# One plain block fewer per FFN, a third pair of rounded weights, and weight sums made by adding transfers

## The chip, the cores and the metric

The kernel runs on one core of a Trainium2 chip. The metric is the time of one execution in device microseconds (us). The engines named below are TensorE (PE in the rows; PEld is its weight load), VectorE (DVE), ScalarE (ACT), GpSimd (POOL) and SyncE (SP), which only sends transfers.

## The reference, cut to what matters

Two layers of a decoder trunk on 512 tokens, with 16 learned meta tokens in front, width 1024. Each layer has an attention part (two groups of heads, one output projection) and a SwiGLU FFN of width 2816. The change touches the FFN:

```python
hn = rmsnorm(h, ffn_norm_g)
ff = jax.nn.silu(jnp.einsum('bld,df->blf', hn, w_gate)) * jnp.einsum('bld,df->blf', hn, w_up)
return h + jnp.einsum('blf,fd->bld', ff, w_down)
```

Everything is float32. `w_gate` and `w_up` are 1024 × 2816 per layer, `w_down` 2816 × 1024.

## The kernel before, in words

**Layout.** The hidden state lies transposed: eight tiles `h[k]` of 128 channels by 528 tokens. Layer 0 works on all 528 columns in two halves of 264; layer 1, whose meta tokens nobody needs after attention, on 512, in plain blocks as one 512-wide matmul and elsewhere as two halves of 256.

**Precision.** A float32 product is made of three matmuls with rounded parts (fp32r): high weight by high x, high weight by low x, low weight by high x. A weight block of 128 columns is loaded into `raw` (or `fraw`) by SP; ACT makes the high part `whi` by a cast (L191 for plain blocks, L869 for units), and VectorE, or POOL in some attention stages, the low part `wlo` by subtraction (L194, L870). Plain blocks use the pair whi/wlo with two buffers, units take turns between whi/wlo and fwhi/fwlo.

**FFN.** The 22 blocks f of 128 FFN columns are grouped in ROUNDS. Those with f < PLAIN are plain: gate and up, each eight k-blocks times three matmuls times two halves, 96 half-width matmuls in all (L217). All others are a `Unit`: gate and up of both token halves as one two-by-two block product by the Winograd form of Strassen's method, with seven products of four k-blocks in place of eight, 84 half-width matmuls (L881). A unit's x-side operands are plain x blocks and four sums (`x_forms`, one call for each k of 0 to 3). `x_forms(k)` scales h[k] on ACT into `S`, makes four sums there on VectorE (L843, L845, L846) and splits them into `th` (ACT) and `tl` (VectorE, L143). All units of a layer share these forms. The weight-side operands come from `make1` to `make4`: the gate block as it is, and sums of halves of `w_gate` and `w_up`, written to `S`, over `fraw` and over `raw` (L915, L916, L922, L929), each followed by cast and subtraction. `need(j)` makes a weight operand when a product starts, and those of the next two jobs with it.

**Rounds.** Products on plain x come first in a unit (its head), then those on the forms. The down projection of the round before (L1016) is laid between the parts of the units. A unit without such a down part leaves its last products (its tail) until behind the head of the next unit.

**Start of an FFN.** The squares for the normalization are inserted at step 4 of the first gate block, `rstd` (the sum over channels on TensorE, L290, and Newton steps on VectorE, L297) at step 12, and the four `x_forms` from step 12 on, nine steps apart.

**Order.** TensorE's order is the order of the program, written by hand. The orders of the other engines are set by the tile scheduler when the program is built, by the order and the priority in which the program gives out the work, and are then fixed. Each engine works through its queue in that order and waits at an instruction until its operands and its buffer are there.

## Time and profile before

| what | value |
|---|---|
| median of three runs (lowest, highest) | 1271.39 us (1270.4, 1271.77) |
| profiled execution, its own time | 1271.32 us |
| its span | 1269.5 us |
| TensorE busy in the span | 1255.6 us |
| VectorE busy | 997.3 us |
| ScalarE busy | 687.7 us |
| GpSimd busy | 264.0 us |

The span is the profiled part of an execution; its own time is 1.8 us longer. The rows of the prediction give a start, or a window, in us from the start of the span. A group's row has its busy time and the number of its instructions. In rows of one engine the two numbers are start and length; since operations of one engine overlap a little at their ends, what one costs its queue is the distance to the next start. Lines (L217) are those of the kernel before.

### The profile page before, as it was taken

The numbers are of one execution on the slowest core, as the hardware profiler recorded it, in microseconds if no ns is written. First come the engines' busy times: TensorE is split into PE (matmuls) and PEld (weight loads), VectorE is DVE, ScalarE is ACT, GpSimd is POOL, SyncE is SP. The second block draws the span as 40 slices with busy tenths as digits, with TensorE's granted clock in tenths as the row PEclk, the third lists the DMA queues.
The fourth block names the chain that finished last, engine by engine and source line by source line (L and its number), as shares of the span: only waits on it lengthen the run. The fifth ranks groups of instructions, "written<-read, shape, count | busy, mean of one in ns | idle before, by whom it ended". The sixth has DMA issues, their size and how long they took to land.

```text
span 1269.5 us, 23615 instructions
## 1 busy us (share of the span) xinstructions
PE 1255.6 (99%) x9271; PEld 1197.8 (94%) x9271; DVE 997.3 (79%) x1843; ACT 687.7 (54%) x1246; POOL 264.0 (21%) x522
## 2 busy tenths in 40 slices
PE   9999999999999999999999999999999999999997
PEld 8999999999999999999999989998789999999996
DVE  7877756779988888887786877567899888888866
ACT  6666545676444444444456665557764444444444
POOL 3355546420000000000025545454100000000000
PEclk9999999999999999999999999999999999999999
DMA  6222232223333333332323232222323333333321
GB/s 217 93 69 86 88 87 73 70 68 114 107 97 100 100 100 101 100 100 84 101 76 119 62 99 83 80 88 68 101 95 120 100 100 100 101 100 100 104 80 67
DMA packets 45680, 120.57 MB, mean 95 GB/s; under 512 B 5360, under 2 KB 12272, under 8 KB 45568
## 3 DMA queue, kind: packets, MB, share of 16 engines
q1 hardware_dynamic: 45104, 118.74, 29.8%
q8 instruction: 73, 1.20, 0.4%
q10 hardware_dynamic: 464, 0.32, 0.1%
q14 instruction: 39, 0.32, 0.1%
HBM read 116.91 MB, written 2.13 MB: 94 GB/s over the span
## 4 chain that ended last, share of the span: by engine, by line
PE 94%; DVE 3%; ACT 2%; DMA 1%; issue 0%; DVEq 0%; ACTq 0%
PE psd L217 30%; PE psa L881 18%; PE psd L1016 14%; PE psd L881 13%; PE psa L217 5%; PE psa L1016 4%; PE psa L418 2%; PE psa L573 2%; PE psa L507 2%; PE psa L730 1%; PE psa L700 1%; PE psa L379 1%; PE psa L290 0%; ACT whi L191 0%; DMA raw<-w_in 0%
## 5 line engine op out<-in xcount | busy, mean ns | idle before, releaser
L194 POOL TENSOR_TENSOR wlo<-raw,whi 128x128 fp32r<-128x128 f32 x504 | 258.8, 548 | 288.5 <-ACT whi L191 288.4
L217 PE MATMUL psd<-xh,whi 128*128 128x264 f32 (+1 forms) x792 | 196.2, 315 | 0.6 <-ACT whi L191 0.6
L217 PE MATMUL psd<-xh,wlo 128*128 128x264 f32 (+1 forms) x792 | 187.2, 304 | 0.0
L217 PE MATMUL psd<-xl,whi 128*128 128x264 f32 (+1 forms) x792 | 186.7, 303 | 0.4 <-DVE xl L320 0.4
L217 PEld LDWEIGHTS psd<-xh,whi 128*128 128x128 f32 x792 | 128.9, 190 | 5.7 <-ACT whi L191 1.3
L217 PEld LDWEIGHTS psd<-xh,wlo 128*128 128x128 f32 x792 | 127.5, 189 | 6.2 <-DVE wlo L194 0.4
L217 PEld LDWEIGHTS psd<-xl,whi 128*128 128x128 f32 x792 | 128.0, 189 | 4.8 <-DVE xl L320 0.8
L191 ACT CAST whi<-raw 128x512 fp32r<-128x512 f32 (+1 forms) x168 | 98.3, 613 | 49.5 <-PE psd L217 37.6
L869 ACT CAST whi<-raw 128x1024 fp32r<-128x1024 f32 (+2 forms) x62 | 54.9, 885 | 51.2 <-PE psd L881 39.9
L869 ACT CAST fwhi<-raw 128x1024 fp32r<-128x1024 f32 (+2 forms) x62 | 55.7, 898 | 47.5 <-PE psd L881 39.9
L1116 POOL TENSOR_TENSOR th<-th,e 128x544 f32<-128x544 f32 x1 | 1.4, 1366 | 359.2 <-DVE e L1136 359.2
L870 DVE TENSOR_TENSOR wlo<-raw,whi 128x1024 fp32r<-128x1024 f32 (+2 forms) x62 | 62.9, 1015 | 12.9 <-ACT whi L869 12.8
L85 POOL MEMSET kl<- 64x528 f32 x2 | 1.1, 534 | 345.4 <-PE psa L881 345.4
L870 DVE TENSOR_TENSOR fwlo<-raw,fwhi 128x1024 fp32r<-128x1024 f32 (+2 forms) x62 | 64.0, 1032 | 10.5 <-ACT fwhi L869 10.3
L881 PE MATMUL psa<-th,whi 128*128 128x264 f32 (+1 forms) x232 | 65.4, 282 | 0.0
L881 PE MATMUL psa<-th,wlo 128*128 128x264 f32 (+1 forms) x232 | 65.4, 282 | 0.0
L881 PE MATMUL psa<-tl,whi 128*128 128x264 f32 (+1 forms) x232 | 65.3, 282 | 0.0
L881 PE MATMUL psa<-th,fwhi 128*128 128x264 f32 (+1 forms) x224 | 63.4, 283 | 0.0
L881 PE MATMUL psa<-tl,fwhi 128*128 128x264 f32 (+1 forms) x224 | 63.3, 283 | 0.0
L881 PE MATMUL psa<-th,fwlo 128*128 128x264 f32 (+1 forms) x224 | 63.2, 282 | 0.0
L527 ACT ACTIVATE probs<-probs,nmax 128x144 f32<-128x144 f32 (+1 forms) x64 | 36.9, 576 | 44.2 <-DVE nmax L514 31.3
L947 ACT COPY e<-psa 128x264 f32<-128x264 f32 (+1 forms) x114 | 42.9, 376 | 28.3 <-PE psa L881 24.1
(340 smaller groups left out, 4030.2 us busy)
## 6 DMA issues: line engine op xcount, KB each, us to landing
raw<-w_in SPq DMA_DIRECT2D x54, 512.0 KB, 3.5
raw<-w_gate SPq DMA_DIRECT2D x44, 512.0 KB, 3.7
fraw<-w_up SPq DMA_DIRECT2D x38, 512.0 KB, 3.5
raw<-w_down SPq DMA_DIRECT2D x64, 256.0 KB, 2.8
raw<-w_out SPq DMA_DIRECT2D x16, 512.0 KB, 3.4
raw<-w_down SPq DMA_DIRECT2D x32, 192.0 KB, 2.4
bc<-cdr SPq DMA_DIRECT2D x16, 264.0 KB, 3.5
raw<-w_up SPq DMA_DIRECT2D x6, 512.0 KB, 3.5
```

The lines of the kernel that those rows point to most:

```text
L191: pin(nc.scalar.copy(hi, job["raw"][:, c0:c1]), pinned)
L194: pin(sub(lo[:, i:i + step], job["raw"][:, c0 + i:c0 + i + step], hi[:, i:i + step].bitcast(F32)), pinned)
L217: nc.tensor.matmul(ps[1][b][:, 0:c1 - c0], w[:, wk, :], x[:, c0:c1], start=(k == 0 and i == 0), stop=(k == n - 1 and i == 2))
L418: nc.tensor.transpose(ps[:, 128 * j:128 * j + 128], src[:, o:o + 128], idt)
L507: nc.tensor.matmul(sc[0:nq, 0:c1 - c0], st["q"][s][:, q0:q0 + nq], kk[:, c0:c1], start=(i == 0), stop=(i == 1))
L527: nc.scalar.activation(pr, pr, AF.Exp, bias=nmax[0:nq], scale=-1.0, accum_out=rsum)
L573: nc.tensor.matmul(po[:, c0:SEQ], v[:, j, :], pp[:, j, META + c0:T], start=(j == 0 and i == 0), stop=(j == 4 and i == 1))
L869: nc.scalar.copy(hi, src)
L870: nc.vector.tensor_sub(lo, src, hi.bitcast(F32))
L881: nc.tensor.matmul(bank()[:, 0:b.shape[-1]], a[:, o + k, :], b, start=(fresh and k == 0 and i == 0), stop=(k == n - 1 and i == 2), skip_gr ...
L947: nc.scalar.copy(self.t["e"][:, i], self.t["x"][:, 0:w])
L1016: nc.tensor.matmul(v[:, 0:c1 - c0], a[:, s * n + k, :], b[:, c0:c1], start=(k == 0 and i == 0), stop=(k == n - 1 and i == 2))
```

## The change

- PLAIN goes from 3 to 2: block f = 2 of both layers becomes a unit. Round 0 has no down projection laid in, so this unit's tail comes behind the head of the first unit of round 1.
- whi/wlo have three buffers in place of two, and plain blocks of the FFN and the second half of the output projection convert the weights of the job after the next as well (`far`).
- `x_forms` has one buffer `S` in place of two, makes two of its sums by one 528-wide operation (the same h block read twice), and takes a negated norm weight from a constant `neg` for the last. The calls are six steps apart in place of nine.
- Two of the four weight sums of a unit are made by transfers: SP loads the lower half of the up block into a buffer of its own, `Sw` (two buffers), and POOL sends the upper half with an addition onto it; a second transfer of POOL adds the upper half of the gate block onto that of the up block in `fraw`. Two VectorE additions per unit go (L915, L922). Signs are turned where the sums now come out with the other sign: in `make2`, `make4` and in the factor of u.

```diff
--- before.py
+++ after.py
-PLAIN = 3
+PLAIN = 2
...
-        return pool.tile([128, NK, 128], F32R, name=tag, tag=tag, bufs=2)
+        return pool.tile([128, NK, 128], F32R, name=tag, tag=tag, bufs=2 if tag[0] == "f" else 3)
...
             job["w"] = [(NK, *(job["own"]() if job["own"] else
-                               [wp.tile([128, NK, 128], F32R, name=i, tag=i) for i in ("whi", "wlo")]))]
+                               [wring(i) for i in ("whi", "wlo")]))]
...
                         convert(j + 1, 4 * half + 4)
+                        if far:
+                            convert(j + 2, 4 * half + 4)
...
             def go():
                 if k == 0:
                     st["t"] = [[fft(f"t{p}{i}", shape=(128, 2, 4, w)) for p in "hl"] for i in range(2)]
-                s = fft("S", F32, (128, 6, w), 2)
+                s = fft("S", F32, (128, 6, w), 1)
...
                 nc.vector.tensor_sub(s[:, 2], s[:, 1], s[:, 0])
-                for i in range(2):
-                    nc.vector.scalar_tensor_tensor(s[:, 3 + i], b[1], g1, s[:, 1 + i], ALU.mult, ALU.subtract)
-                nc.vector.scalar_tensor_tensor(s[:, 5], a[1], g1, s[:, 4], ALU.mult, ALU.subtract)
+                nc.vector.scalar_tensor_tensor(s[:, 3:5], b[1].unsqueeze(1).broadcast_to([128, 2, w]), g1, s[:, 1:3],
+                                               ALU.mult, ALU.subtract)
+                nc.vector.scalar_tensor_tensor(s[:, 5], a[1], neg[:, l * HB + k:l * HB + k + 1], s[:, 4], ALU.mult, ALU.add)
                 th, tl = (t[:, k % 2] for t in st["t"][k // 2])
                 split(th, tl, s[:, 2:6])
...
                         nc.sync.dma_start(self.t[n], src[l, self.f])
+                    s = self.t["s"] = fft("Sw", F32, (128, NK, 128), 2)
+                    nc.sync.dma_start(s[:, HB:NK], w_up[l, self.f][:, HB:NK])
+                    nc.gpsimd.dma_start(s[:, HB:NK], w_up[l, self.f][:, 0:HB], accum_op=ALU.add)
+                    nc.gpsimd.dma_start(self.t["b"][:, 0:HB], w_gate[l, self.f][:, 0:HB], accum_op=ALU.add)
...
             def make2(self, hi, lo):
-                a, b = self.t["a"], self.t["b"]
-                s = self.t["s"] = fft("S", F32, (128, NK, 128), 2)
-                nc.vector.tensor_add(s[:, HB:NK], b[:, 0:HB], b[:, HB:NK])
-                nc.vector.tensor_sub(s[:, 0:HB], s[:, HB:NK], a[:, 0:HB])
-                splits(hi, lo, s)
+                a, s = self.t["a"], self.t["s"]
+                nc.vector.tensor_add(s[:, 0:HB], s[:, HB:NK], a[:, 0:HB])
+                nc.scalar.activation(hi, s, AF.Copy, scale=-1.0)
+                nc.vector.scalar_tensor_tensor(lo, s, -1.0, hi.bitcast(F32), ALU.mult, ALU.subtract)
 
             def make3(self, hi, lo):
-                a, b = self.t["a"], self.t["b"]
-                nc.vector.tensor_sub(b[:, 0:HB], a[:, 0:HB], b[:, 0:HB])
-                splits(hi, lo, b)
+                splits(hi, lo, self.t["b"])
 
             def make4(self, hi, lo):
                 a, s = self.t["a"], self.t["s"]
-                nc.vector.tensor_sub(a[:, HB:NK], a[:, HB:NK], s[:, 0:HB])
+                nc.vector.tensor_add(a[:, HB:NK], a[:, HB:NK], s[:, 0:HB])
                 splits(hi, lo, a[:, HB:NK])
...
-                nc.vector.scalar_tensor_tensor(u[:, c], sg[:, c], RSC, st["R"][:, c], ALU.mult, ALU.mult)
+                nc.vector.scalar_tensor_tensor(u[:, c], sg[:, c], -RSC, st["R"][:, c], ALU.mult, ALU.mult)
...
-                    steps += dense_steps(w_gate[l, f], [(0, xs, NK, QC, g_done(f) if f else held.append)], banks=f == 1)
-                    steps += dense_steps(w_up[l, f], [(0, xs, NK, QC, u_done(f))])
+                    steps += dense_steps(w_gate[l, f], [(0, xs, NK, QC, g_done(f) if f else held.append)], banks=f == 1, far=True)
+                    steps += dense_steps(w_up[l, f], [(0, xs, NK, QC, u_done(f))], far=True)
...
-            steps.insert(NK + 4 + 9 * i, x_forms(i))
+            steps.insert(NK + 4 + 6 * i, x_forms(i))
```

Lines of the changed kernel are some two higher than before (L843 becomes L845, L881 becomes L883). The next rows are VectorE's, in the order of its queue, at the first call of `x_forms`; `S` is its buffer, `th`/`tl` its result, `h_77` and so on the hidden state, `Sw` the new buffer. Before:

```order
L143 TENSOR_TENSOR sql<-ss,sqh 128x528
L194 TENSOR_TENSOR wlo<-raw,whi 128x512 x3
L843 TENSOR_TENSOR S<-S 128x264
L845 SCALAR_TENSOR_TENSOR S<-h_77,vec,S 128x264 x2
L194 TENSOR_TENSOR wlo<-raw,whi 128x512
L846 SCALAR_TENSOR_TENSOR S<-h_77,vec,S 128x264
L843 TENSOR_TENSOR S<-S 128x264
L845 SCALAR_TENSOR_TENSOR S<-h_78,vec,S 128x264 x2
L846 SCALAR_TENSOR_TENSOR S<-h_78,vec,S 128x264
L143 TENSOR_TENSOR tl_4304<-S,th_4303 128x1056
```

With the change:

```order
L143 TENSOR_TENSOR sql<-ss,sqh 128x528
L194 TENSOR_TENSOR wlo<-raw,whi 128x512 x3
L845 TENSOR_TENSOR S<-S 128x264
L194 TENSOR_TENSOR wlo<-raw,whi 128x512
L846 SCALAR_TENSOR_TENSOR S<-h_77,vec,S 128x528
L919 TENSOR_TENSOR Sw<-Sw,raw 128x512
L848 SCALAR_TENSOR_TENSOR S<-h_77,neg,S 128x264
L919 TENSOR_TENSOR Sw<-Sw,raw 128x512
L921 SCALAR_TENSOR_TENSOR fwlo<-Sw,fwhi 128x1024
L299 TENSOR_TENSOR nwt<-R 128x528
L143 TENSOR_TENSOR tl_4315<-S,th_4314 128x1056
```

Two weight sums (L919, reading `Sw`) and a low part (L921) now stand between the form's first operation and its `tl`, and the next form's L845 only behind that.

At the last of the four calls, before:

```order
L845 SCALAR_TENSOR_TENSOR S<-h_80,vec,S 128x264 x2
L143 TENSOR_TENSOR tl_4306<-S,th_4305 128x1056
L825 SCALAR_TENSOR_TENSOR tq<-psd,R 128x528
L194 TENSOR_TENSOR wlo<-raw,whi 128x512
L826 TENSOR_TENSOR tq<-tq,sg 128x528
L846 SCALAR_TENSOR_TENSOR S<-h_80,vec,S 128x264
L194 TENSOR_TENSOR wlo<-raw,whi 128x512
L143 TENSOR_TENSOR al_4487<-tq,ah_4486 128x528
L915 TENSOR_TENSOR S<-fraw 128x512
L143 TENSOR_TENSOR tl_4306<-S,th_4305 128x1056
L817 SCALAR_TENSOR_TENSOR sg<-psd,R 128x528
```

With the change:

```order
L930 TENSOR_TENSOR raw<-raw,Sw 128x512
L143 TENSOR_TENSOR al_4503<-tq,ah_4502 128x528
L930 TENSOR_TENSOR raw<-raw,Sw 128x512
L143 TENSOR_TENSOR tl_4317<-S,th_4316 128x1056
L872 TENSOR_TENSOR wlo<-raw,whi 128x512
L872 TENSOR_TENSOR wlo<-fraw,whi 128x1024
L845 TENSOR_TENSOR S<-S 128x264
L846 SCALAR_TENSOR_TENSOR S<-h_80,vec,S 128x528
L848 SCALAR_TENSOR_TENSOR S<-h_80,neg,S 128x264
L919 TENSOR_TENSOR Sw<-Sw,raw 128x512
L143 TENSOR_TENSOR tl_4317<-S,th_4316 128x1056
```

The last `tl` is now preceded by two sums over `raw` (L930), two low parts, and another L919, which is the next unit's. From the first L845 to this row there are 41 instructions; before, between the same two places, 36 rows of this list, some standing for two.

SP's transfers at the start of the first FFN, before (L158 are plain blocks):

```order
L158 DMA raw<-w_gate 128x1024
L158 DMA raw<-w_up 128x1024
L158 DMA raw<-w_gate 128x1024
L158 DMA raw<-w_up 128x1024
L905 DMA fraw<-w_up 128x1024 x2
L158 DMA raw<-w_gate 128x1024
L158 DMA raw<-w_up 128x1024
L905 DMA raw<-w_gate 128x1024
```

With the change:

```order
L158 DMA raw<-w_gate 128x1024
L158 DMA raw<-w_up 128x1024
L158 DMA raw<-w_gate 128x1024
L158 DMA raw<-w_up 128x1024
L907 DMA raw<-w_gate 128x1024
L907 DMA fraw<-w_up 128x1024
L909 DMA Sw<-w_up 128x512
L907 DMA fraw<-w_up 128x1024
L909 DMA Sw<-w_up 128x512
L907 DMA raw<-w_gate 128x1024
```

Between the second plain block's weights and the first unit's own gate nothing changes place; behind them stand four loads in place of two, and POOL's queue, which sent nothing before, holds in turn the additions to `fraw` (L911) and to `Sw` (L910), two for each unit.

On TensorE, where the third plain block began behind the last product of f = 1, there now begins the head of a unit on plain x (24 matmuls, then its first product on `th` and `tl`).

More of the change, by code (lines that the diff above doesn't have):

```diff
@@ L195, in convert, with dense_steps @@
             job["split"] = c1
-    def dense_steps(src, parts, pool=False, banks=False, ahead=(1, 4), own=None, wait=None):
+    def dense_steps(src, parts, pool=False, banks=False, ahead=(1, 4), own=None, wait=None, far=False):
         j = len(jobs)
@@ L791, in out_proj @@
         return sum([dense_steps(w_out[l, rnd, m2], [(4 * s, xs, 4, cols, add_h(2 * m2 + s, real)) for s in range(2)],
-                                rnd == 0 or m2 < 2, rnd == 1 and m2 == 1) for m2 in range(NK // 2)], [])
+                                rnd == 0 or m2 < 2, rnd == 1 and m2 == 1, far=rnd == 1) for m2 in range(NK // 2)], [])
     def ffn(l, st, real, last):
@@ L1100, in square_b @@
                 if m == 0:
-                    t = fft("S", F32, (128, 6, w), 2)
+                    t = fft("S", F32, (128, 6, w), 1)
                     fin["one"] = [t[:, i, 0:nb] for i in range(3)]
@@ L1222, in ffn @@
         return steps
+    neg = const.tile([128, DEPTH * HB], F32, name="neg")
+    for i in range(DEPTH):
+        nc.vector.tensor_scalar_mul(neg[:, HB * i:HB * i + HB], vec[:, V_FFN + NK * i + HB:V_FFN + NK * i + NK], -1.0)
     gf = const.tile([128, NK], F32, name="gf")
```

## The prediction

> **What bounds the kernel now.** I read first the line of busy times and the shares of the chain that ended last.
>
> ```profile
> span 1269.5 us, 23615 instructions
> ...
> PE 1255.6 (99%) x9271; PEld 1197.8 (94%) x9271; DVE 997.3 (79%) x1843; ACT 687.7 (54%) x1246; POOL 264.0 (21%) x522
> ...
> PE 94%; DVE 3%; ACT 2%; DMA 1%; issue 0%; DVEq 0%; ACTq 0%
> ```
>
> TensorE is busy 99% and is 94% of the chain. So the time falls only if matmuls go, and rises if anything lets TensorE stand. The profiled execution took 1271.32 us, 1.8 more than its span, and the median is 1271.39: I add my sum to that. Then I read the stages around the edit, as windows (us, then busy time of PE, PEld, DVE, ACT, POOL, granted clock, DMA share, GB/s).
>
> ```profile
> 255.00:277.00 22.00, 22.00 (x179) 21.68 (x178) 13.67 (x23) 14.07 (x25) 6.70 (x13) 1.00 0.16 49
> 277.00:331.00 54.00, 54.00 (x447) 53.86 (x446) 53.56 (x90) 36.03 (x56) 0.00 (x0) 1.00 0.36 115
> 331.00:646.00 315.00, 315.00 (x2594) 315.00 (x2593) 254.20 (x377) 144.04 (x206) 2.60 (x11) 1.00 0.31 98
> 902.00:922.00 20.00, 19.62 (x85) 15.36 (x84) 19.80 (x35) 14.28 (x26) 0.00 (x0) 1.00 0.47 155
> 922.00:955.00 33.00, 33.00 (x174) 28.10 (x173) 32.37 (x51) 20.81 (x30) 0.00 (x0) 1.00 0.32 105
> ```
>
> Two things are to be seen. Where units follow one another (331 to 646) TensorE is full and VectorE is busy 254 of 315 us. But at the start of each FFN (277 to 331, and 902 to 955 in layer 1) VectorE is itself full, 53.56 of 54 us and 52.17 of 53. There the four x-side forms are made, and there the change puts its new unit. VectorE works in the order of its program, so a form that comes late stops TensorE.
>
> **What it saves on TensorE.** A plain block is 96 half-width matmuls in layer 0, a unit is 84. From the chain, in order of time (start, length, what):
>
> ```profile
> 300.68 5.79 PE psa L217 x48
> ...
> 533.80 2.91 PE psa L1016 x24
> ...
> 539.64 2.93 PE psd L1016 x24
> ...
> 613.96 2.91 PE psa L1016 x24
> ...
> 929.97 16.67 PE psd L217 x72
> ...
> 1118.56 2.78 PE psd L1016 x12
> ...
> 1227.08 2.76 PE psd L1016 x12
> ```
>
> In layer 0, 48 plain matmuls take 5.79 us, a block 11.59. From 533.80 to 613.96 lie five units with their down products, 16.03 us each; without 48 down products (2.91 + 2.93) a unit is 10.19. Saved: 1.40. In layer 1 a plain block is 48 matmuls at 16.67 / 72, 11.11 us; seven units in 108.52 us, 15.50 each, less 24 down products (twice 2.78), are 9.94. Saved: 1.17. Together **−2.6 us**, if every operand is there in time.
>
> **What it costs at the head of the FFN.** Before, the third plain block stands between the first gate and the first product that reads a form. These are rows of TensorE and VectorE around it (start, length).
>
> ```profile
> 288.12 0.41 PE L217 MATMUL psd<-xh,whi 128*128 128x264 f32 x2
> 297.10 0.41 PE L290 MATMUL psa<-sqh,ones 128*128 128x264 f32 x2
> 297.59 0.41 PE L217 MATMUL psd<-xh,whi 128*128 128x264 f32 x2
> 280.26 0.76 DVE L320 SCALAR_TENSOR_TENSOR xl<-h,vec,xh 128x528 fp32r<-128x528 f32 x1
> 280.94 0.70 DVE L340 TENSOR_TENSOR ss<-ss,sq 128x528 f32<-128x528 f32 x1
> 293.81 1.90 DVE L194 TENSOR_TENSOR wlo<-raw,whi 128x512 fp32r<-128x512 f32 x3
> 295.61 0.44 DVE L843 TENSOR_TENSOR S<-S 128x264 f32<-128x264 f32 x1
> 295.96 0.90 DVE L845 SCALAR_TENSOR_TENSOR S<-h,vec,S 128x264 f32<-128x264 f32 x2
> 296.76 0.70 DVE L194 TENSOR_TENSOR wlo<-raw,whi 128x512 fp32r<-128x512 f32 x1
> 317.29 1.25 DVE L143 TENSOR_TENSOR tl<-S,th 128x1056 fp32r<-128x1056 f32 x1
> 318.46 0.70 DVE L817 SCALAR_TENSOR_TENSOR sg<-psd,R 128x528 f32<-128x528 f32 x1
> 319.08 1.22 DVE L870 TENSOR_TENSOR wlo<-raw,whi 128x1024 fp32r<-128x1024 f32 x1
> 320.21 0.69 DVE L916 TENSOR_TENSOR S<-S,raw 128x512 f32<-128x512 f32 x1
> ```
>
> *When the forms are needed.* FFN 0 begins at 288.12. With two plain blocks TensorE has 192 plain matmuls (23.2 us), the sum of squares (297.10 to 297.59, 0.49) and 24 products of the new unit on plain x (2.9): it wants the first form at 314.7 and, nine matmuls behind it (0.12 us each), the fourth, whose low part it reads at about 315.9. Before, with 96 matmuls more ahead of it, the last form had until about 327 and was there at 318.5.
>
> *When they will be there.* VectorE's order (shown above, at the change) has, from the first form's first operation to the last form's low part, 41 instructions: to the forms' own are now added the new unit's weight sums and conversions and the next unit's, since the program gives them out in the same stretch. I price them by the distance from one start to the next: 264 columns 0.35 (295.61 to 295.96), with a column scalar 0.40 (0.80 for two), 512 columns 0.60 (293.81 to 295.61, three), 528 0.62, 528 with a scalar 0.68 (280.26 to 280.94), 1024 1.13, 1056 1.17. That is 7 × 0.60 + 5 × 1.13 + 4 × 1.17 + 9 × 0.62 + 4 × 0.68 + 8 × 0.35 + 4 × 0.40 = 27.2 us, against 22.85 for the same stretch before (295.61 to 318.46). Nothing ahead of it moves in a way that frees VectorE earlier: the conversions that now run one job further ahead fill its pauses before 277, where it was busy 13.67 of 22 us, and TensorE already had no gap there. So the stretch starts at 295.6 as before and, with no wait at all, ends at 322.8: **6.9 us late**. The merged form operation (one of 528 for two of 264, 0.68 for 0.80) is already in the sum; 0.12 × 4 is all it gives.
>
> *Waits within it.* VectorE's queue now holds three L919 rows that read a sum made by an adding transfer. Before, nothing there waited on POOL's queue.
>
> ```profile
> 287.80 0.90 SPq L905 DMA_DIRECT2D fraw<-w_up  x2
> ...
> DMA to landing us min/median/max: 4.3/4.3/4.3
> ...
> raw<-w_down SPq DMA_DIRECT2D x64, 256.0 KB, 2.8
> ```
>
> At 287.80 two loads of 512 KB went out and landed after 4.3 us. At this place there are now four, 1.5 MB: by bytes 6.5 us, to 294.3. The adding transfers follow, four of them on POOL's one queue. No row shows one. An ordinary 256 KB load takes 2.8 us (lower bound: it also reads what it adds to); twice that, 5.6, is the upper. I take 4.0, nearer 4.3 for two transfers that share the engines, with 1 us from one issue to the next. Then the first sum lands at about 297.9 and the second at 300.6, against VectorE's arrival at 297.2 and some 298.4: 0.7 + 2.2. The third is worse placed: its load needs the first sum's buffer, free only when the second L930 row is done; then come 2.8 for the load and 4.0 for the addition, 6.8 in all, and VectorE has 4.9 us of other rows up to it: 1.8, with 0.3 for cast and hand-over. So about **5.0 us** more in layer 0. The bounds: if the additions landed as soon as they were sent, loads, buffer exchange and hand-overs would still cost 2.3; at 5.6 us, issued 2 us apart, the three waits grow by 1.6, 2.6 and 2.6, to some 12.
>
> Layer 1 has the same order, of 39 instructions:
>
> ```profile
> 911.86 0.40 PE L217 MATMUL psd<-xh,whi 128*128 128x512 f32 x1
> 919.71 0.42 DVE L843 TENSOR_TENSOR S<-S 128x256 f32<-128x256 f32 x1
> ```
>
> By the same prices 26.6 us from 919.71, to 946.3; the fourth form is wanted at 911.86 + 22.2 + 0.5 + 2.8 + 1.2 = 938.6. That is **7.7 late**, and 6.1 for waits (the three transfers 4.7, the last form's cast and hand-over 1.4).
>
> Sum: 6.9 + 5.0 + 7.7 + 6.1 − 2.6 = +23.1, **1294.5 us**.
>
> The Trainium skill, page "DMA: Bandwidth & Descriptors", section "Anatomy of one DMA — SWDGE (gpsimd) path", fits a transfer issued by POOL as 2.0 us and its bytes by 436 GB/s: 2.6 for 256 KB, without addition. By that estimate the waits shrink by about 2 us a layer and the time is about 1290. No run here shows such a transfer yet.
>
> **What costs or gives nothing.** Two VectorE additions of 512 fewer per unit are 1.2 us of 16: VectorE has 61 us of pause in 315 there, TensorE none, so nothing comes of it; if that cover were gone it would be worth 1.2 us a unit. A unit's own sums are called for two jobs ahead; its transfers have some 8 us before a product misses them, twice the 4.0, so additions pass unseen there. They add 0.75 MB to some 1.57 MB a unit: by the share of 0.31 about 0.46, which 902 to 922 already bore. The third pair of rounded weights could fill the 0.38 us that TensorE stands in 902 to 922, at most; I leave that out.
>
> **The rivals.** *The queue is in time*: the last form's low part by 315.9 and 938.6, TensorE never stands, and only the saving is left: 1271.4 − 2.6 = 1268.8, faster. It needs 6.9 us less work on VectorE ahead of that row than the order has; for it speaks only that each form's rows are scattered among weight work that may not all be ahead. *Additions land at once*: only the lower bounds of the waits stay, 2.3 and 2.4 (its cast 1.2 among them): 6.9 + 2.3 + 7.7 + 2.4 − 2.6 = +16.7, 1288. For it: the first loads are sent some 9 us ahead of VectorE's arrival; against it: no row shows an addition at no price. *Additions slow or one after another*: POOL's queue sends the next only when the last has landed. The second and the third sum then each stand behind another addition, 4 us each: about +8 a layer, 1311. *The clock*: TensorE now stands for 4 to 6 us at a time. After the last matmul the page shows what follows:
>
> ```profile
> 5.60:9.60 4.00, 4.00 (x18) 4.00 (x19) 3.33 (x7) 3.60 (x8) 0.00 (x0) 1.00 1.05 395
> 10.00:14.00 4.00, 4.00 (x35) 4.00 (x34) 4.00 (x8) 4.00 (x8) 0.00 (x0) 1.00 1.04 360
> 1262.00:1266.00 4.00, 0.00 (x0) 0.00 (x0) 3.51 (x7) 1.50 (x4) 0.00 (x0) 0.97 0.57 195
> 1266.00:1269.50 3.50, 0.00 (x0) 0.00 (x0) 0.08 (x1) 0.00 (x0) 0.00 (x0) 0.50 0.64 217
> ```
>
> The clock is at half 4 us after the end of work, and a start from rest runs 18 matmuls in 4 us where 35 are usual. A stall of that length in each layer, with some 4 us of work at half speed behind it, costs +2 each: 1298.5. The Trainium skill, "TensorE: Matmul & The Clock Gate", section "HAM oscillation — how this bites in real kernels", has it that an idle window of about 3.4 us brings the half clock; the rows of the end agree, with under 4.
>
> **How the numbers follow.** Late forms with waits as summed: 0.43 (1294.5). With the clock on top: 0.16 (1298.5). Additions at once: 0.18 (1288). Slow additions: 0.13 (1311). In time: 0.07 (1268.8). Partly in time, within 0.2% (2.5 us, what a measurement of this kernel can just tell): 0.03. So slower 0.90, same 0.03, faster 0.07. The range takes in the unseen transfer's bounds: down to 1284 (additions at once, and 4 us less by rows cheaper than priced), up to 1315 (additions one after another, with the clock on top).
>
> **What would show it.** Right: TensorE busy in 300 to 335 and 930 to 955 with some 12 to 14 us of pause each, released by VectorE's `tl` rows and ACT's `th`; VectorE full there, idle ahead of its L919 rows on a transfer into Sw; units after it without pauses, 16 and 15.5 us each. Wrong: pauses spread over all units (then additions are slower than 8 us), or no pause ahead of the first form product (then the queue held), or the x-form stretch well under 27 us.

## The result, and the profile after

The changed kernel takes 1319.99 us (median of four runs, 1319.42 to 1323.36) against 1271.03 for the kernel before. The ratio is 1.039, with a 95% interval of 1.0378 to 1.0402: slower by 49 us. Slower was forecast, but by 23; the time lies beyond the stated range too, which ended at 1315.

The page of the changed kernel, its first two lines, its queues and the adding transfers:

```profile
span 1318.7 us, 23921 instructions
...
PE 1266.4 (96%) x9295; PEld 1206.9 (92%) x9295; DVE 957.0 (73%) x1771; ACT 690.4 (52%) x1252; POOL 336.9 (26%) x602
...
q1 hardware_dynamic: 50864, 129.23, 31.0%
q0 software_dynamic: 11520, 20.98, 10.0%
...
fraw<-w_gate POOLq DMA_DIRECT2D x40, 256.0 KB, 5.0
Sw<-w_up POOLq DMA_DIRECT2D x40, 256.0 KB, 6.0
```

TensorE stands for 52 us of the span, where it stood for 14. VectorE has 40 us less to do, as was meant, and nothing comes of it. POOL's queue (q0) carries 21 MB and holds the engines for 10.0% of the span; SP's (q1) carries six times as much in 31.0%. An adding transfer of 256 KB takes 5 to 6 us from issue to landing in the median, where the plain 256 KB load of the prediction took 2.8.

Where the time went is read from four points: the first matmul of FFN 0, of layer 1, of FFN 1, and the end of the span (all in us).

| kernel | FFN 0 starts | FFN 0 | attention, layer 1 | FFN 1 and the end | span |
|---|---|---|---|---|---|
| before | 288.12 | 357.78 | 265.96 | 357.64 | 1269.5 |
| changed | 291.70 | 379.63 | 267.24 | 380.13 | 1318.7 |
| difference | +3.6 | +21.9 | +1.3 | +22.5 | +49.2 |

Most lies in the two FFNs, at their starts: of the stages by window (PE, PEld, DVE, ACT, POOL busy, then granted clock, DMA share, GB/s) the two starts are full of pauses, and where units follow one another there are none.

```profile
300.00:355.00 55.00, 37.26 (x271) 36.16 (x270) 34.11 (x50) 23.71 (x32) 3.81 (x5) 0.81 0.43 105
...
500.00:646.00 146.00, 146.00 (x1202) 146.00 (x1202) 103.59 (x152) 63.09 (x91) 12.11 (x14) 1.00 0.50 129
...
922.00:985.00 63.00, 47.11 (x206) 37.67 (x204) 48.80 (x74) 32.90 (x50) 6.12 (x7) 0.87 0.49 130
```

VectorE's queue in FFN 0, from the first form's first row to the last form's low part (start, length, and in brackets the idle time before it and what ended it):

```profile
299.21 0.42 DVE L845 TENSOR_TENSOR S<-S 128x264 f32<-128x264 f32 x1
...
304.95 0.69 DVE L919 TENSOR_TENSOR Sw<-Sw,raw 128x512 f32<-128x512 f32 x1 [4.04 <-DMA Sw<-w_up]
...
309.81 0.69 DVE L919 TENSOR_TENSOR Sw<-Sw,raw 128x512 f32<-128x512 f32 x1 [3.76 <-DMA Sw<-w_up]
...
338.23 0.69 DVE L919 TENSOR_TENSOR Sw<-Sw,raw 128x512 f32<-128x512 f32 x1 [4.92 <-DMA Sw<-w_up]
338.84 1.25 DVE L143 TENSOR_TENSOR tl<-S,th 128x1056 fp32r<-128x1056 f32 x1
```

The stretch runs from 299.21 to 340.0, 40.8 us. Three waits for adding transfers make 12.7 of it; the rest, 28.1, is VectorE's own rows and half a microsecond of other waits. The additions onto `Sw` that these three rows wait for were sent from POOL's queue at 297.64, 299.51 and 330.70:

```profile
297.64 0.96 POOL L910 DMA_DIRECT2D Sw<-w_up  x1
...
299.51 0.86 POOL L910 DMA_DIRECT2D Sw<-w_up  x1
...
330.70 0.85 POOL L910 DMA_DIRECT2D Sw<-w_up  x1 [1.83 <-DVE wlo L872]
```

They landed 7.3, 10.3 and 7.5 us after their issue. TensorE's answer, in its own rows:

```profile
316.96 0.78 PE L217 MATMUL psd<-xh,whi 128*128 128x264 f32 x2 [7.17 <-DVE sg L819]
...
329.96 0.39 PE L883 MATMUL psa<-tl,fwhi 128*128 128x264 f32 x1 [1.37 <-DVE tl L143]
...
334.47 0.59 PE L883 MATMUL psa<-th,fwhi 128*128 128x264 f32 x1 [4.01 <-ACT th L142]
340.15 0.59 PE L883 MATMUL psa<-tl,fwhi 128*128 128x264 f32 x1 [5.09 <-DVE tl L143]
...
343.62 0.42 PE L883 MATMUL psa<-tl,whi 128*128 128x264 f32 x1
343.83 0.41 PE L883 MATMUL psa<-th,wlo 128*128 128x264 f32 x1
344.06 0.30 PE L883 MATMUL psa<-th,whi 128*128 128x264 f32 x1
344.20 0.28 PE L883 MATMUL psa<-tl,whi 128*128 128x264 f32 x1
```

The 7.17 is the up product of f = 1, whose bank is freed by row L819; that row stands behind the first two waits in VectorE's queue. The others are the third and fourth form. After each long pause matmuls go 0.22 us apart for 3 to 4 us, and then 0.12 again. FFN 1 shows the same, with waits of 4.80, 2.11 and 2.55 us ahead of its three L919 rows, a pause of 5.2 us before the up product of f = 1, and its last low part at 983.59.

### The profile page after: what moved, and what is told of

Same layout as the page of the kernel before. It is cut to its first block, busy times and chain, and to the rows that moved or that the text cites. A ratio compares the mean times of both kernels' runs of the same rounds, so it can differ in the third digit from the quotient of the medians.

```text
span 1318.7 us, 23921 instructions
## 1 busy us (share of the span) xinstructions
PE 1266.4 (96%) x9295; PEld 1206.9 (92%) x9295; DVE 957.0 (73%) x1771; ACT 690.4 (52%) x1252; POOL 336.9 (26%) x602
## 3 DMA queue, kind: packets, MB, share of 16 engines
q0 software_dynamic: 11520, 20.98, 10.0%
## 5 line engine op out<-in xcount | busy, mean ns | idle before, releaser
L217 PE MATMUL psd<-xh,whi 128*128 128x264 f32 (+1 forms) x744 | 185.4, 318 | 12.9 <-DVE sg L819 7.2
L217 PE MATMUL psd<-xh,wlo 128*128 128x264 f32 (+1 forms) x744 | 175.7, 305 | 0.0
L217 PE MATMUL psd<-xl,whi 128*128 128x264 f32 (+1 forms) x744 | 175.4, 304 | 0.1
L217 PEld LDWEIGHTS psd<-xh,whi 128*128 128x128 f32 x744 | 122.5, 193 | 18.0 <-issue 13.0
L217 PEld LDWEIGHTS psd<-xh,wlo 128*128 128x128 f32 x744 | 120.8, 191 | 5.2
L217 PEld LDWEIGHTS psd<-xl,whi 128*128 128x128 f32 x744 | 121.3, 191 | 3.9 <-DVE xl L322 0.5
L911 POOL DMA_DIRECT2D fraw<-w_gate x40 | 34.7, 868 | 348.2 <-DMA fraw<-w_up 124.7
L910 POOL DMA_DIRECT2D Sw<-w_up x40 | 34.9, 874 | 254.2 <-DVE sg L959 84.2
L919 DVE TENSOR_TENSOR Sw<-Sw,raw 128x512 f32<-128x512 f32 x40 | 27.7, 692 | 83.9 <-DMA Sw<-w_up 65.6
L883 PE MATMUL psa<-th,fwhi 128*128 128x264 f32 (+1 forms) x232 | 66.6, 287 | 12.6 <-ACT th L142 12.5
L883 PE MATMUL psa<-tl,fwhi 128*128 128x264 f32 (+1 forms) x232 | 66.8, 288 | 8.5 <-DVE tl L143 8.5
L883 PE MATMUL psa<-th,whi 128*128 128x264 f32 (+1 forms) x248 | 70.5, 284 | 0.0
L883 PE MATMUL psa<-tl,whi 128*128 128x264 f32 (+1 forms) x248 | 70.3, 284 | 0.0
L883 PE MATMUL psa<-th,wlo 128*128 128x264 f32 (+1 forms) x248 | 70.1, 283 | 0.0
L883 PE MATMUL psa<-th,fwlo 128*128 128x264 f32 (+1 forms) x232 | 66.0, 284 | 0.0
```

The source lines that it names most:

```text
L217: nc.tensor.matmul(ps[1][b][:, 0:c1 - c0], w[:, wk, :], x[:, c0:c1], start=(k == 0 and i == 0), stop=(k == n - 1 and i == 2))
L883: nc.tensor.matmul(bank()[:, 0:b.shape[-1]], a[:, o + k, :], b, start=(fresh and k == 0 and i == 0), stop=(k == n - 1 and i == 2), skip_gr ...
L910: nc.gpsimd.dma_start(s[:, HB:NK], w_up[l, self.f][:, 0:HB], accum_op=ALU.add)
L911: nc.gpsimd.dma_start(self.t["b"][:, 0:HB], w_gate[l, self.f][:, 0:HB], accum_op=ALU.add)
L919: nc.vector.tensor_add(s[:, 0:HB], s[:, HB:NK], a[:, 0:HB])
```

## The experiments

Each kernel's time, its ratio to the kernel before on the same chip, and the four points (the columns after the start of FFN 0 are differences from the kernel before, in us):

| run | time, us | ratio, 95% | FFN 0 starts | FFN 0 | attention | FFN 1 and end |
|---|---|---|---|---|---|---|
| sums_dve | 1295.9 | 1.018 to 1.021 | 292.31 | +8.7 | +1.4 | +9.3 |
| plain3 | 1280.4 | 1.006 to 1.009 | 293.35 | +1.0 | +1.4 | +2.6 |
| two_pairs | 1301.4 | 1.022 to 1.025 | 287.52 | +15.4 | +0.1 | +14.8 |
| pool_copy | 1306.4 | 1.026 to 1.030 | 291.85 | +14.7 | +1.3 | +16.7 |
| before_plain2 | 1290.5 | 1.014 to 1.017 | 287.92 | +9.7 | 0.0 | +10.3 |
| before_far | 1276.4 | 1.003 to 1.006 | 291.93 | +0.5 | +1.2 | −0.4 |
| keep_clock | 1319.7 | 1.037 to 1.040 | 292.94 | +21.4 | +1.2 | +21.4 |
| pool_lows | 1286.5 | 1.011 to 1.014 | 287.02 | +8.8 | 0.0 | +6.9 |
| sums_two_pairs | 1290.7 | 1.014 to 1.017 | 288.04 | +8.9 | +0.1 | +11.1 |
| one_add | 1313.5 | 1.032 to 1.035 | 292.63 | +17.5 | +1.4 | +17.5 |

### Without the adding transfers

```diff
-                    s = self.t["s"] = fft("Sw", F32, (128, NK, 128), 2)
-                    nc.sync.dma_start(s[:, HB:NK], w_up[l, self.f][:, HB:NK])
-                    nc.gpsimd.dma_start(s[:, HB:NK], w_up[l, self.f][:, 0:HB], accum_op=ALU.add)
-                    nc.gpsimd.dma_start(self.t["b"][:, 0:HB], w_gate[l, self.f][:, 0:HB], accum_op=ALU.add)
...
+                s = self.t["s"] = fft("Sw", F32, (128, NK, 128), 2)
+                nc.vector.tensor_add(s[:, HB:NK], b[:, 0:HB], b[:, HB:NK])
...
+                nc.vector.tensor_add(b[:, 0:HB], a[:, 0:HB], b[:, 0:HB])
```

> The changed kernel with all four weight sums on VectorE again (no transfer into Sw, no adding transfer); two plain blocks, one S, the third pair and the forms' places stay. Theory 'both' (VectorE's own rows make the forms late, and the waits for additions come on top): the L919-type waits of 12.7 us (layer 0) and 9.5 us (layer 1) go, the forms stay late by VectorE's rows with about 2 x 0.6 us more a unit; each FFN still loses some 8 to 9 us net and the attention part stays 4.9 us longer: 1271 + 15.5 + 4.9 = about 1291. Rival 'additions alone': without them the forms are in time, 1271 + 4.9 - 2.6 = about 1273. Rival 'queue alone': the additions only wait where VectorE is late anyway, the time stays above 1310.

Measured 1295.9, 5 us above what "both" expected and far from the two rivals. Each FFN is still 9 us longer than before: the adding transfers, with the loads into `Sw` that they need, made 13 of the 22. VectorE's stretch in FFN 0 now has no such wait:

```profile
299.81 0.42 DVE L845 TENSOR_TENSOR S<-S 128x264 f32<-128x264 f32 x1
...
326.58 1.26 DVE L143 TENSOR_TENSOR tl<-S,th 128x1056 fp32r<-128x1056 f32 x1
```

It ends at 327.75, 27.9 us long, of 43 rows. FFN 0 starts at 292.31 here, so the low part was wanted at 320.1 (27.8 later, as in the prediction): 7.6 late, by VectorE's own rows alone. Less the 1.4 saved that is 6.2 of the 8.7; behind TensorE's pause the granted clock is 0.60 from 328 to 332, worth some 1.6 more, and the last microsecond was not followed.

### Three plain blocks with the rest of the change

```diff
-PLAIN = 2
+PLAIN = 3
```

> The changed kernel with three plain blocks as before; additions, one S, the third pair stay. Theory 'both': the third plain block gives the forms 11.6 us in layer 0 and 11.1 in layer 1 more time; most of the loss at the FFN's start goes, the 4.9 us of the attention part stay: 1276, and up to 1285 if the additions' waits of 9 to 13 us don't all fit into the 11.6. Rival 'additions alone', with the waits wherever the block stands: 1300 or more, with TensorE's pauses in units all over the FFN.

Measured 1280.4. The pauses of the FFN's start are gone, with all additions in place; what stays is mainly 6.7 us in the attention parts. So the additions cost 1.0 and 2.6 us an FFN, not 13, where the forms have the time of a third plain block; in the following units they pass nearly unseen. The forecast of the prediction that steady units have cover enough holds.

### Two pairs of rounded weights in the changed kernel

```diff
-        return pool.tile([128, NK, 128], F32R, name=tag, tag=tag, bufs=2 if tag[0] == "f" else 3)
+        return pool.tile([128, NK, 128], F32R, name=tag, tag=tag, bufs=2)
...
-                                rnd == 0 or m2 < 2, rnd == 1 and m2 == 1, far=rnd == 1) for m2 in range(NK // 2)], [])
+                                rnd == 0 or m2 < 2, rnd == 1 and m2 == 1, far=False) for m2 in range(NK // 2)], [])
...
-banks=f == 1, far=True)
+banks=f == 1)
```

(The same for the up blocks.)

> The changed kernel with two whi/wlo pairs and no conversion further ahead; the rest as changed. Theory: the third pair frees the raw buffers earlier, the weight loads then stand ahead of the bc broadcast in attention, and that costs the 3.6 us before the first FFN and 1.3 us before the second: FFN 0 starts at 288.1 again and FFN 1 266.0 us after layer 1's first matmul; with fewer conversions in the FFN's start the time falls by 5 to 10 us: 1310 to 1315. Rival (the delay comes from the adding transfers' queue or from the new constant): FFN 0 still starts at 291.7 and the time stays at 1318 to 1322.

Measured 1301.4, further down than expected. FFN 0 starts at 287.5 again, and the FFNs are 6.4 and 7.7 us shorter too, which I had put at 5 in all at most. In VectorE's queue of FFN 0 the L919 row of the second unit stands later, and the 3.76 us that it waited are gone; the row that waits for the third addition stands behind the last low part instead of ahead of it:

```profile
323.86 0.68 DVE L919 TENSOR_TENSOR Sw<-Sw,raw 128x512 f32<-128x512 f32 x1
...
328.31 1.26 DVE L143 TENSOR_TENSOR tl<-S,th 128x1056 fp32r<-128x1056 f32 x1 [1.14 <-ACT th L142]
...
332.20 0.69 DVE L919 TENSOR_TENSOR Sw<-Sw,raw 128x512 f32<-128x512 f32 x1 [2.63 <-DMA Sw<-w_up]
```

Converting further ahead had put sums of later units ahead of forms, where their waits hold the forms up. The first L919 still waits 4.32 us here, for its unit's gate load. The third pair and the earlier conversion go together in this run; they were not tried apart.

### The transfers without the addition

```diff
-                    nc.gpsimd.dma_start(s[:, HB:NK], w_up[l, self.f][:, 0:HB], accum_op=ALU.add)
-                    nc.gpsimd.dma_start(self.t["b"][:, 0:HB], w_gate[l, self.f][:, 0:HB], accum_op=ALU.add)
+                    nc.gpsimd.dma_start(s[:, HB:NK], w_up[l, self.f][:, 0:HB])
+                    nc.gpsimd.dma_start(self.t["b"][:, 0:HB], w_gate[l, self.f][:, 0:HB])
```

> The changed kernel with POOL's two transfers of a unit as plain copies: the addition onto the loaded half is left out, so two weight sums hold one summand only; bytes, queue and waits are the same. Theory 'bandwidth' (an addition holds the transfer engines twice as long per byte, 159 against 314 GB/s by the queues' shares): four copies land some 5 us earlier than the 13 us after the first issue, the waits fall from 12.7 and 9.5 to 5 to 7 a layer, the time to about 1305 to 1310. Rival 'POOL's queue sends one at a time, 3 to 4 us each, whatever it carries': landings and time as in the changed kernel, 1318 to 1321.

Measured 1306.4, as the bandwidth theory had it. With the addition left out two of its weight sums hold one summand only, so nothing but its times is of use. The queue and the landings:

```profile
q0 software_dynamic: 6400, 20.98, 5.2%
...
fraw<-w_gate POOLq DMA_DIRECT2D x40, 256.0 KB, 3.5
Sw<-w_up POOLq DMA_DIRECT2D x40, 256.0 KB, 4.2
```

The same 20.98 MB hold the engines for 5.2% of the span as copies and 10.0% as additions, and land 1.5 to 1.8 us sooner in the median. At the start of FFN 0 the first two onto `Sw` land after 3.8 and 5.7 us in place of 7.3 and 10.3, and the three waits fall from 12.7 to 5.3 us. So POOL's queue alone does not make the additions slow; more than half of the waits comes with the addition, which keeps the engines twice as long per byte at a place where they are full. But that is not all that these transfers cost: the FFNs are 8.7 and 9.3 us longer than before with no such transfer, 14.7 and 16.7 with copies, 21.9 and 22.5 with additions. Of some 13 us each, 7.2 and 5.8 go with the addition; 6.0 and 7.4 stay with the copies, the loads into `Sw` among them. In the changed kernel, by windows:

```profile
292.00:296.00 4.00, 4.00 (x35) 4.00 (x35) 4.00 (x7) 3.07 (x6) 0.00 (x0) 1.00 0.94 321
296.00:300.00 4.00, 4.00 (x36) 4.00 (x35) 4.00 (x8) 1.31 (x3) 3.27 (x4) 1.00 0.93 253
300.00:304.00 4.00, 4.00 (x36) 4.00 (x35) 0.91 (x2) 0.85 (x2) 0.38 (x1) 1.00 0.84 184
304.00:308.00 4.00, 4.00 (x36) 4.00 (x35) 1.10 (x2) 2.32 (x3) 0.00 (x0) 1.00 1.04 243
```

For 16 us the transfer engines are busy 84% and more: five loads of SP, four additions, and from 298.75 three loads more.

### One addition a unit in place of two

```diff
-                    nc.gpsimd.dma_start(self.t["b"][:, 0:HB], w_gate[l, self.f][:, 0:HB], accum_op=ALU.add)
...
+                nc.vector.tensor_add(b[:, 0:HB], a[:, 0:HB], b[:, 0:HB])
```

> The changed kernel with only one adding transfer a unit (onto Sw); the sum over fraw is VectorE's again. Theory 'the transfer engines are full there, and additions queue behind one another' (issue to landing 4.2, 7.3, 9.4, 10.3 us for the first four): the two additions that are left at the FFN's start land about 4.2 and 6 to 7 us after issue, the first L919's wait falls from 4.0 to 1 or 2 us, the second's from 3.8 to about 1, and the FFNs lie between 8.7 (no additions) and 21.9 (both): about +13 to +17 each, the time 1303 to 1310. Rival 'an addition onto Sw takes 6 to 7 us by itself': waits and time as in the changed kernel, 1318 to 1321.

Measured 1313.5 (1311 to 1316), less of a gain than expected. The first two additions onto Sw, issued at 298.67 and 300.60, end these waits:

```profile
303.32 0.69 DVE L918 TENSOR_TENSOR Sw<-Sw,raw 128x512 f32<-128x512 f32 x1 [1.48 <-DMA Sw<-w_up]
...
306.83 0.69 DVE L918 TENSOR_TENSOR Sw<-Sw,raw 128x512 f32<-128x512 f32 x1 [1.81 <-DMA Sw<-w_up]
```

POOL issues them at the same places in the FFN as in the changed kernel (6.0 and 8.0 us from its start). They land after 4.6 and 6.2 us, as forecast, where those of the changed kernel took 7.3 and 10.3, and these two waits fall about as forecast; but the third is still 2.62, and VectorE has one more row a unit. Each FFN stays 17.5 us longer, half a microsecond outside the stated 13 to 17, and the time lies 3 us above the stated 1303 to 1310. The rival, by which the waits would have stayed, is refuted: with half the additions in flight the same two land 3 to 4 us sooner. With the copies it says that two causes share the waits, the other transfers in flight and the time that one addition holds the engines.

### Two plain blocks alone

```diff
-PLAIN = 3
+PLAIN = 2
```

in the kernel before, with nothing else.

> The kernel before with PLAIN 2 and nothing else of the change (two pairs, two S, all sums on VectorE, forms nine steps apart). Theory 'VectorE's queue': by its order the last form's tl is late by 7 to 9 us a layer here too, without any adding transfer; less 2.6 saved, with 1 us for a low part late beside it: about 1288, pauses of TensorE before form products only. Rival 'the new parts (one S, third pair, additions) make all of the loss': two plain blocks are enough for the forms, 1268.8.

Measured 1290.5: slower by 19 us without any other part of the change. The waits of TensorE that are new (waited for, total, times, longest):

```profile
PE psa L881 <- ACT th L142: 8.2, 2, 4.4
PE psa L881 <- DVE tl L143: 1.6, 2, 0.8
...
PE psa L881 <- DVE fwlo L870: 1.5, 2, 0.8
PE psa L881 <- ACT fwhi L869: 1.4, 1, 1.4
```

They stand before form products and the weights of those products, made by VectorE and the cast ahead of it; two more, of 0.9 us each, stand before down products. This is the rival "the queue is in time" refuted in its plainest form.

### The third pair alone

```diff
+                        if far:
+                            convert(j + 2, 4 * half + 4)
```

with three buffers for whi/wlo, in the kernel before.

> The kernel before with the third whi/wlo pair and the conversion of the job after next, nothing else. Theory 'the load ahead of bc': the third load of w_in stands ahead of the bc loads in SP's queue and waits there for its buffer; bc lands 2 to 4 us later, TensorE waits for nmax some 2.5 to 4 us and goes on at half clock for a while: FFN 0 starts 3.6 to 5 us later than 288.1, FFN 1 another 1.4 later, the FFNs themselves as before: 1276 to 1278. Rival 'the delay needs the other parts (a constant more, other sums)': 1271, FFN 0 at 288.1.

Measured 1276.4, the whole loss in the attention parts. SP's queue in the first attention, before, and with the third pair:

```profile
24.52 6.59 SPq L158 DMA_DIRECT2D raw<-w_in  x2
36.83 0.81 SPq L497 DMA_DIRECT2D bc<-cdr  x2
41.00 0.33 SPq L158 DMA_DIRECT2D raw<-w_in  x1
```

```profile
25.10 13.15 SPq L158 DMA_DIRECT2D raw<-w_in  x3
38.30 1.05 SPq L499 DMA_DIRECT2D bc<-cdr  x2
41.73 0.33 SPq L158 DMA_DIRECT2D raw<-w_in  x1
...
PE psa L509 <- DVE nmax L516: 2.6, 1, 2.6
```

A third load of w_in now stands ahead of the two bc loads in SP's order and ends at 38.25, since it waits for its buffer; bc goes out 1.5 us later, shares the engines with that load and lands after 4.2 us in place of 3.2. TensorE waits 2.6 us for nmax (the row maxima, which need bc), where it waited 0.5; behind that pause the granted clock is 0.57 from 44 to 48, worth 1.7 us. These two are nearly all of the 3.8 us by which FFN 0 starts later.

### The clock

```diff
+                        if busy and k == n - 1 and i == 1:
+                            for _ in range(20):
+                                nc.tensor.matmul(bank()[:, 0:w], hi[:, o, :], nought[:, 0:w], start=False, stop=False, skip_group_check=True)
```

> The changed kernel with 20 more matmuls (weights by a tile of zeros, added to the running sum) in layer 0 between the high and the low part of the fourth form in the new unit's first form product, where TensorE stood 5.09 us and then ran at half clock until 344. Theory 'the clock costs about 2 us a layer on top of the stall': the 20 matmuls fit into the pause (4.4 us at half speed), the 18 matmuls behind it go at 0.12 us in place of 0.22, the time falls by 1.5 to 2 us: about 1318. Rival 'clock costs nothing of its own' : time as in the changed kernel or up to 1 us longer, 1320 to 1321. Rival 'the busy state does not bring the clock back': 1320 and the matmuls behind at 0.22.

The edit is at work in that one product of layer 0 alone. Measured 1319.7, no different from the changed kernel. In TensorE's rows the 20 matmuls do what they were to do:

```profile
335.37 0.59 PE L886 MATMUL psa<-th,fwhi 128*128 128x264 f32 x1 [4.01 <-ACT th L142]
335.76 3.86 PE L885 MATMUL psa<-nought,fwhi 128*128 128x264 f32 x20
341.22 0.39 PE L886 MATMUL psa<-tl,fwhi 128*128 128x264 f32 x1 [1.61 <-DVE tl L143]
341.45 0.28 PE L886 MATMUL psa<-th,fwlo 128*128 128x264 f32 x1
341.57 0.29 PE L886 MATMUL psd<-th,fwhi 128*128 128x264 f32 x1
```

The granted clock is 0.50 from 332 to 336 and 1.00 from 340 to 344, and behind the 20 the matmuls go 0.12 us apart at once. Counted from the FFN's start (1.24 us later here, in an attention that the edit doesn't touch), the products on forms are done 1.9 us sooner than in the changed kernel. But FFN 0 as a whole is only 0.5 shorter, no more than FFN 1, which the edit doesn't touch, differs by itself (1.1). Of the 1.9 us 1.0 is still there 190 us into the FFN; 0.6 went in one wait for VectorE on the way, and where the rest went was not followed. The half clock is real and its local price is as stated; how much of it reaches the FFN's end, between nothing and 1 us here, this run can't tell.

### Two blocks with VectorE relieved

```diff
-PLAIN = 3
+PLAIN = 2
+POOLS = ('g0', 'u0', 'g1', 'u1')
...
-                nc.vector.tensor_sub(s[:, 2], s[:, 1], s[:, 0])
+                nc.gpsimd.tensor_sub(s[:, 2], s[:, 1], s[:, 0])
...
-                    steps += dense_steps(w_up[l, f], [(0, xs, NK, QC, u_done(f))])
+                    steps += dense_steps(w_up[l, f], [(0, xs, NK, QC, u_done(f))], f"u{f}" in POOLS)
...
-                    tails = [u]
+                    u.last()
+                    steps += u.tail()
...
-            steps.insert(NK + 4 + 9 * i, x_forms(i))
+            steps.insert(NK + 4 + 6 * i, x_forms(i))
```

in the kernel before (the gate blocks get the same argument as the up blocks).

> The kernel before with PLAIN 2, the forms six steps apart, and VectorE relieved at the FFN's start: the low parts of the two plain blocks (four weights) and the forms' first difference go to POOL, which rests there; the first unit's tail follows its own middle, so that its result is earlier for the down product. All sums stay on VectorE, two pairs, two S. Theory 'VectorE's queue sets the forms': some 10 rows of 0.6 and four of 0.35 us leave VectorE, the forms are there within 1 us of need, TensorE pauses 1 to 2 us in all and the saving of 2.6 us shows in part: 1269 to 1271. Rival 'the forms' own chain (ACT, VectorE, ACT, VectorE) is too long for two plain blocks': pauses before form products stay, 1280 or more.

Measured 1286.5: the expectation missed by 15 us, and the kernel is slower than before. The waits before form products did go, against the rival too, whose time (1280 or more) it has all the same: another wait took their place, and VectorE and POOL slow each other down. A wait of TensorE, POOL's row, and two of VectorE's:

```profile
PE psd L218 <- DVE sg L818: 9.7, 2, 5.3
...
282.05 12.11 POOL L195 TENSOR_TENSOR wlo<-raw,whi 128x128 fp32r<-128x128 f32 x16 [10.83 <-ACT whi L192]
...
287.86 0.97 DVE L341 TENSOR_TENSOR ss<-ss,sq 128x528 f32<-128x528 f32 x1
288.76 0.69 DVE L785 TENSOR_TENSOR h<-psd,h 128x528 f32<-128x528 f32 x1
```

POOL's subtractions take 0.76 us here, 0.55 on average before. VectorE's sum of two 528-wide tiles takes 0.90 to the next start, where the same row took 0.62 without POOL at work. The Trainium skill, page "SBUF — State Buffer", section "Who interferes with whom", says that a VectorE operation with two inputs in SBUF contends with a GpSimd operation that reads SBUF, for a port that one of them holds at a time; these rows agree, and the row with an input in PSUM (L785) keeps its 0.62. With the forms now ahead of the normalization in VectorE's queue, row L818, which frees the bank of the first gate block, became the late one.

### Closing the square

> The changed kernel with all four sums on VectorE and two whi/wlo pairs: of the change stay PLAIN 2, one S, the merged form operation, the forms six steps apart. It closes the square of additions and third pair. Theory 'the third pair only hurts attention where no addition is waited for': attention as before (FFN 0 at 287.5 to 288.1), the FFNs 8 to 10 us longer than before as with the sums alone back on VectorE: about 1289 to 1291. Rival 'the third pair lengthens the FFN by 6 to 7 us whatever makes the sums': FFNs only 2 us longer than before, about 1276.

This is the kernel without additions (first experiment) with two pairs (third). Measured 1290.7, as expected from the first theory: FFNs 8.9 and 11.1 us longer, attention as before. So, per FFN:

| | two pairs | three pairs |
|---|---|---|
| sums on VectorE | +8.9, +11.1 | +8.7, +9.3 |
| sums by additions | +15.4, +14.8 | +21.9, +22.5 |

The third pair costs an FFN nothing by itself, and 6.4 to 7.7 us where additions are waited for. No version that was tried beats the kernel before; by the prediction's sum, the most to be had from one plain block fewer is 2.6 us.

## Why the prediction was right and wrong

**The bound and the sign held.** TensorE was full, and the time rose because something let it stand: forms late by VectorE's queue. Two plain blocks alone cost 19 us. One pause was not in the forecast, 7.2 us in FFN 0 and 5.2 in FFN 1 before the up product of f = 1: the rows of the normalization stand behind the first two waits in VectorE's queue too. TensorE still reached the last two forms before they were there, so it adds nothing to the loss.

**The priced rows held.** 27.2 us were forecast for VectorE's 41 rows in FFN 0; in the changed kernel the stretch took 28.1 outside the waits for additions, and without additions 27.9, which is what the prices give for its 43 rows (three sums of 0.60 more, one low part of 1.13 less). The lateness by rows, forecast as 6.9 in FFN 0, was 7.6 there, and the FFNs are 9 us longer without any addition; the half clock behind the pause is part of the difference.

**The failed step is the waits for the additions: "I take 4.0, nearer 4.3 for two transfers that share the engines", which gave 0.7 + 2.2 + 1.8.** The three landed 7.3, 10.3 and 7.5 us after their issue; the waits were 4.0, 3.8 and 4.9, 12.7 us for 4.7 forecast, and 9.5 in FFN 1 for 4.7. When the first was issued had been forecast well: 297.64 is 5.9 us into the FFN, and 297.9 less 4.0 in the forecast is 5.8. I had counted the loads ahead of the additions, but let each addition then have the engines nearly to itself. 4.0 is near what one takes with no other addition ahead of it: 4.2 for the very first, onto `fraw`, and 4.6 for the first onto `Sw` where a unit has only one. But here four were in flight within 3 us, each held the engines twice as long per byte as a copy, and three loads sent from 298.75 on shared them. At the third the prediction also misread the order: its load went out behind the first L930 row (327.54), not the second, and the wait was longer all the same. The upper bound that the prediction gave for these waits in layer 0, about 12, was reached; the value chosen from between the bounds was the error. The fit of the Trainium skill, page "DMA: Bandwidth & Descriptors", section "Anatomy of one DMA — SWDGE (gpsimd) path" (2.6 us for 256 KB by estimate), lay further off still: in the median they took 3.5 and 4.2 as copies on POOL's queue, 5.0 and 6.0 as additions.

**A term was missing: 4.9 us in the attention parts.** The prediction said that the conversions moved ahead only fill VectorE's pauses, and costed the third pair at nothing. The step that was left out is SP's queue: a load that may be issued earlier stands earlier in that queue, ahead of the bc loads, and waits there. The third pair alone shows all of it. Of the 25.5 us by which the forecast fell short, the waits for additions are 12.8 and the attention parts 4.9.

**And the third pair was not independent of the additions.** It put L919 rows of later units ahead of the forms. The prediction counted these rows, but as the change's own; going back to two pairs takes 6.4 to 7.7 us from each FFN.

**The rivals.** "In time" (1268.8) fell with two plain blocks alone. "Additions at once" (1288) is near the 1290 to 1296 of the kernels without additions. "One after another" (1311) had the right size for the waits of FFN 0, 8 us more than forecast, but not the right mechanism: POOL issued all four before the first had landed. That additions in flight hold each other up is right: with one a unit in place of two they land 3 to 4 us sooner. "The clock" was rightly priced where it happens, 2 us a layer. Whether it belongs in the sum in full stays open: taking it away behind the second stall of FFN 0 changed the time by no measurable amount.

**By size:** FFN 0 in the changed kernel: last low part at 340.0, wanted at 291.70 + 27.8 = 319.5, 20.5 late, less 1.4 saved 19.1; with the clock behind it, 1.9 at most, 21.0 of 21.9 measured. FFN 1: 984.7 against 965.3, 19.4 late, less 1.2 saved 18.2; with at most 2.1 of clock (985 to 990 at 0.58) 20.3 of 22.5. What remains, 1 to 4 us an FFN, was not followed further; 1.5 us of pauses stand in 985 to 1100.

## What to carry to other kernels

When work is taken off an engine that isn't the bound, look at the one stretch where that engine is full, and price every row ahead of the result that the bound waits for; the average share says nothing about it. A transfer that has to land before a queue goes on is priced by all that is in flight at that moment, not by its duration alone, and where the nearest row lies far from the operation, the upper bound belongs in the forecast's centre as much as the lower. A buffer more lets transfers be issued earlier, and so moves them in their queue: look at what they now stand ahead of.

## What the runs showed of the hardware

- An adding transfer holds the transfer engines twice as long per byte as a copy: 10.0% of 1318.7 us against 5.2% of 1305.9 for the same 20.98 MB.
- Additions in flight together land later: the first two onto `Sw` after 4.6 and 6.2 us with one addition a unit, after 7.3 and 10.3 with two.
- VectorE rows with two SBUF inputs and POOL's subtractions slow each other: 0.90 for 0.62 us, and 0.76 for 0.55.
- Matmuls that only add zeros bring the clock back: 20 of them in a pause of 5 us, and the next ones go 0.12 us apart in place of 0.22.
- A pause of TensorE of 2.6 us was followed by the half clock: 0.57 in the 4 us that begin 1.1 us after it.
